# Attention over the memory: the query and output products run by token half, with held weight tiles

## The chip, the cores and the metric

The kernel runs on one core of a Trainium2 chip. The metric is the device time of one execution in microseconds (us), from runs of the whole program; a separate profiled execution gives the trace that is read below. The engines named are PE (TensorE's products; PEld is its loading of the stationary operand), DVE (VectorE), ACT (ScalarE), POOL (GpSimd) and SP (SyncE, which here only issues transfers).

## The reference, cut to what matters

The program is a stack of two models over 256 tokens of width 1024. The first has two layers, and each of them ends its mixer with an attention over a memory of 256 rows, followed by a feed-forward block:

```python
def memory_cross_attention(h, m, w_q, w_kv, q_norm, k_norm, w_o):
    q = rms_norm(to_heads(h @ w_q, XM_HEADS), q_norm)      # h is 256x1024, w_q 1024x512
    k, v = jnp.split(m @ w_kv, 2, axis=-1)
    k = rms_norm(to_heads(k, XM_HEADS), k_norm)
    v = to_heads(v, XM_HEADS)
    sc = jnp.einsum('bhqd,bhkd->bhqk', q, k).astype(jnp.float32) * (XM_HEAD_DIM ** -0.5)
    p = jax.nn.softmax(sc, axis=-1)
    o = jnp.einsum('bhqk,bhkd->bhqd', p.astype(v.dtype), v)
    return from_heads(o) @ w_o                              # w_o is 512x1024
```

There are 4 heads of width 128. `h` is the normed residual stream, and the result is added to the stream `x`. Everything else of the program (two mixers, four feed-forward blocks and the second model) stands before and after it and is not edited.

## The kernel before, in words

**Halves and parts.** The 256 tokens are two halves of 128, h0 and h1 (the loop variable `h` in the code). A matrix product in float32 precision is made from three products of shorter floats: each operand is split into a high and a low part (`xh`, `xl` of the activations, `wh`, `wl` of the weights), and `dense` issues low by high, high by low and high by high for each block of 128 contracted columns. The stationary operand is a 128x128 block of activations, the moving one 512 weight columns.

**Weight tiles.** `weights` loads a tile of two blocks (128x1024 floats, 512 KB) into one of 4 buffers `wr` and splits it: ACT copies the high part (L159), DVE subtracts it from the raw tile for the low part (L160). Without a room of its own the pair goes to the pools `wh` (3 buffers) and `wl` (2 buffers), which all products share. A buffer is free for the next tile when the last product that reads it is done.

**Order in `dense`.** It takes one tile after the other, and for each tile does h0, then h1. Both accumulators (the two PSUM banks `d`) stay open to the last tile, then `done(0)` and `done(1)` are called. A list of rooms, `apart`, changes this for the last `len(apart)` tiles: they are all prepared first, and h0 runs through all of them and calls `done(0)`, and only then h1. A room is a pair of pool names, or None for `wh` and `wl`. Two other places of the kernel use this already.

**The stage.** `memory_attention` norms and transposes `x` (`norm_T`: DVE L292, PE L231, ACT L234, DVE L235, in two column halves i=0 and i=1 for each token half), makes the queries with `dense` on `xm_w_q` (8 blocks, 4 tiles, 24 products for each half) and gives each half to `heads_T`: ACT L819 takes the accumulator, ACT L504 squares it, DVE L506, DVE L243 and POOL L244 make the norm, PE L516 transposes the four heads into the one PSUM bank `t`, and `evac` (ACT L120 or DVE L122) takes them out. Then for h0 and h1, and two heads at a time: scores (PE L480 into a bank `pC0` to `pC3`), the maximum (DVE L563, L566), exponentials (ACT L877), weighing (DVE L704), transposes of the probabilities (PE L757) with their evacuation (ACT L120, DVE L124), and the product with V (PE L480 into the one bank `o`, tile `po`). `split` (ACT L699, DVE L700) takes `po` out into `opK` and `olK`. `out_proj` then multiplies by `xm_w_o` (4 blocks, 2 tiles) for the columns n0=0 and again for n0=512; its `done` (DVE L682) adds the result to `x`. The norm of the feed-forward block follows.

**Buffers.** The layers run in the scopes `m0` and `m1`, which hold 4 buffers of 4 KB a partition under the name `lb4`. In `m0` they carry the two tiles of the memory, two query tiles and a key tile of the mixer; in `m1` the memory and the keys of the four head groups. All of those are read for the last time before the mixer's own output product ends. The feed-forward block's scope lays its own pools over the same bytes: the pools of a scope lie one behind the other in the order in which they are listed.

```python
        "ffn": (dict(g4=2, b2=6, b1=6, b05=2, lb1=1, opX=2, olX=2, op=6, ol=6, wh=4, wl=4, s=10, ls=16),
...
        "m0": (dict(g4=2, b2=6, lb4=4, lb2=7, lb8=1, b1=1, b05=1, chains=4, b2C0=3, b2C1=3, olK=2, b2C3=3, b2O=2, opK=2, b2C2=3,
...
                dict(t=1, o=1, d=2, tK="t", pC0=1, pC1=1, pC2=1, pC3=1, aC0="pC0", tC0="pC0", aC1="pC1", tC1="pC1", aC2="pC2",
```

**What sets the order.** The program is traced in source order, and a list scheduler with its own estimate of durations fixes the order of instructions on each engine when the kernel is built: at each step an engine gets the ready instruction that stands first in the source (a `later` block moves this by so many places). On the chip each engine runs its list in that order and waits where an operand is not there.

Of the kernel before, what the change touches and what calls it, by code (L numbers as in the profile page):

```python
# [487 lines left out]
class Mix1(Core):  # L488
# [187 lines left out]
            filler()  # L676
        self.out_proj(get, I["ab_w_out"][0])

    def out_proj(self, get, w):
        for n0 in (0, 512):  # L680
            def done(h, ps, s=slice(n0, n0 + 512)):
                self.nc.vector.tensor_tensor(self.x[h][:, s], ps, self.x[h][:, s], op=OP.add)  # L682
            self.dense(get, w, n0, 512, done)

    def heads_out(self, och, po, pT, V, heads, d, nb):

# [168 lines left out]
    def memory_attention(self, layer, kv, V):  # L855
        nc, I = self.nc, self.I
        gain = self.row_gain(I["xm_norm"][layer], 1024)

        qg = self.gains_T(I["xm_q_norm"][layer], I["xm_k_norm"][layer], 128)
        qr = [self.l(4) for _ in range(2)]  # L860
        xT = self.norm_T(self.x, gain)
        qT = [self.l(512) for _ in range(2)]
        qv = [t.rearrange("p (h t) -> p h t", h=4) for t in qT]
        self.dense(xT, I["xm_w_q"][layer], 0, 512, lambda h, ps: self.heads_T(ps, xT.r[h], qv[h], qr[h], qg))
        put, get = self.operand(4, [("opK", 4)])
        for h in range(2):
            with self.on("O"):
                po = self.p("o")
            pov = po.rearrange("p (b t) -> p b t", b=4)
            och = Chain(self)  # L870
            for g in (0, 2):
                with self.chain():
                    ps, sv, nmax, pr, pv = self.scores([g, g + 1], lambda i: qv[h][:, i], lambda i: kv[:, i], 256,
                                                       qr[h][:, g:g + 2])
                    sums = self.t(2)
                    for i in range(2):
                        nc.scalar.activation(pv[:, i], sv[:, i], AF.Exp, bias=nmax[:, i:i + 1], scale=qr[h][:, g + i:g + i + 1],  # L877
                                             accum_out=sums[:, i:i + 1])
                    nc.vector.reciprocal(sums, sums)
                    self.weigh(pv, sums)  # L880
                    pT = self.probs_T(h, [pv[:, 0], pv[:, 1]], 2)
                    self.heads_out(och, pov, pT, V, (g, g + 1), 128, 2)
            self.split(put, h, 0, pov)
        self.out_proj(get, I["xm_w_o"][layer])


    def mla(self, filler):
# [1009 lines left out]
```

## Time and profile before

| what | us |
|---|---|
| median of 3 runs (lowest, highest) | 1979.38 (1978.55, 1986.77) |
| the profiled execution, its own time | 1978.56 |
| its span from the first to the last instruction | 1976.9 |
| memory attention of layer 0, from the last query product to the first output product | 365.6 to 382.1 |
| the same of layer 1 | 925.4 to 942.0 |

Places in the trace are given in us from the start of the span. An idle time is given at the instruction that ended it, with the instruction that released it behind an arrow. Products overlap in PE, so that the duration of one is longer than the distance to the next.

### The profile page before, as it was taken

How to read it: one execution, taken by the hardware profiler on the slowest of the kernel's cores; microseconds unless marked ns; L12 is line 12 of the kernel's file. 1: busy time of each engine (PE TensorE's matmuls, PEld its weight loads, DVE VectorE, ACT ScalarE, POOL GpSimd, SP SyncE). 2: the span in 40 equal slices, each digit the busy share in tenths (PEclk: the TensorE clock that was granted, in tenths of full speed). 3: DMA queues.
4: the chain of work that ended last, by engine and by line, in shares of the span. 5: the costliest groups of instructions: out<-in, count | busy, mean ns of one | idle time of the engine just before them, and what ended most of it. 6: DMA issues, size and time to landing. Idle time of an engine off the chain costs nothing.

```text
span 1976.9 us, 35277 instructions
## 1 busy us (share of the span) xinstructions
PE 1889.1 (96%) x14108; PEld 1678.2 (85%) x14108; DVE 1251.0 (63%) x1999; ACT 996.7 (50%) x1611; POOL 191.2 (10%) x270
## 2 busy tenths in 40 slices
PE   8999999899999999899999999998999998998998
PEld 7998778799989987677999888777998796778996
DVE  5665865766566657676666567665555777466555
ACT  5554656554445545665554456453554464434542
POOL 0000401000000001320000013210000214110000
PEclk9999999999999999899999999999999999999999
DMA  7666443466556656234566664313666654025664
GB/s 231 194 214 224 141 144 104 129 199 193 193 194 196 194 195 194 86 107 149 159 193 193 214 152 127 111 44 118 197 194 194 172 163 152 13 75 179 194 193 139
DMA packets 158645, 319.17 MB, mean 161 GB/s; under 512 B 28944, under 2 KB 49680, under 8 KB 158480
## 3 DMA queue, kind: packets, MB, share of 16 engines
q1 hardware_dynamic: 157888, 315.79, 51.0%
q8 instruction: 111, 1.82, 0.4%
q0 software_dynamic: 160, 0.52, 0.1%
q10 hardware_dynamic: 432, 0.60, 0.1%
q14 instruction: 54, 0.44, 0.1%
HBM read 315.82 MB, written 1.05 MB: 160 GB/s over the span
## 4 chain that ended last, share of the span: by engine, by line
PE 47%; DVE 5%; issue 4%; DMA 1%; POOL 1%; ACT 1%; SPq 0%; DVEq 0%; POOLq 0%; ACTq 0%
PE pd L480 21%; PE pd L217 5%; PE pd L218 5%; PE pd L219 5%; PE po L480 2%; PE pr L480 1%; PE ppC L480 1%; DVE wl L160 1%; PE pr L1477 1%; PE pq L1477 1%; PE pg L480 1%; PE pn L480 1%; PE pg L1247 0%; PE pt L516 0%; DMA wr<-in_w_out_dram 0%
## 5 line engine op out<-in xcount | busy, mean ns | idle before, releaser
L160 DVE TENSOR_TENSOR wl<-wr,wh 128x1024 fp32r<-128x1024 f32 (+2 forms) x557 | 675.0, 1214 | 398.6 <-PE pd L218 125.4
L159 ACT ACTIVATE wh<-wr 128x1024 fp32r<-128x1024 f32 (+2 forms) x557 | 584.4, 1051 | 551.8 <-PE pd L480 203.9
L480 PE MATMUL pd<-opX,wl 128*128 128x256 f32 x2112 | 585.3, 278 | 2.1 <-DVE s L243 1.0
L480 PE MATMUL pd<-olX,wh 128*128 128x256 f32 x2112 | 585.1, 277 | 0.3 <-DVE olX L235 0.2
L480 PE MATMUL pd<-opX,wh 128*128 128x256 f32 x2112 | 584.4, 277 | 0.0
L480 PEld LDWEIGHTS pd<-opX,wl 128*128 128x128 f32 x2112 | 398.3, 189 | 2.9 <-ACT opX L234 2.2
L480 PEld LDWEIGHTS pd<-olX,wh 128*128 128x128 f32 x2112 | 398.6, 189 | 0.7 <-DVE olX L235 0.7
L480 PEld LDWEIGHTS pd<-opX,wh 128*128 128x128 f32 x2112 | 398.4, 189 | 0.0
L218 PE MATMUL pd<-wl,op 128*128 128x512 f32 (+4 forms) x952 | 366.8, 386 | 4.5 <-DVE wl L160 4.2
L219 PE MATMUL pd<-wh,op 128*128 128x512 f32 (+4 forms) x952 | 363.0, 382 | 0.0
L217 PE MATMUL pd<-wh,ol 128*128 128x512 f32 (+4 forms) x952 | 342.9, 386 | 6.8 <-DVE ol L235 5.7
L217 PEld LDWEIGHTS pd<-wh,ol 128*128 128x128 f32 x952 | 178.6, 189 | 42.1 <-DVE ol L235 6.9
L218 PEld LDWEIGHTS pd<-wl,op 128*128 128x128 f32 x952 | 179.8, 189 | 40.6 <-DVE wl L160 7.7
L219 PEld LDWEIGHTS pd<-wh,op 128*128 128x128 f32 x952 | 179.7, 189 | 32.5
L244 POOL TENSOR_TENSOR ls<-s,cf 128x1 f32<-128x1 f32 (+2 forms) x30 | 26.6, 887 | 720.9 <-DVE s L243 711.0
L357 DVE TENSOR_TENSOR b<-pd,b 128x256 f32<-128x256 f32 x132 | 55.9, 424 | 62.2 <-ACT b L356 44.2
L244 POOL TENSOR_TENSOR s<-s,cf 128x1 f32<-128x1 f32 (+2 forms) x22 | 22.4, 1019 | 434.2 <-DVE s L243 432.9
L356 ACT ACTIVATE b<-b 128x256 f32<-128x256 f32 x88 | 36.8, 418 | 46.6 <-DVE b L355 46.6
L361 DVE TENSOR_TENSOR ol<-b,op 128x512 fp32r<-128x512 f32 x66 | 45.4, 688 | 18.0 <-ACT op L360 18.0
L360 ACT ACTIVATE op<-b 128x512 fp32r<-128x512 f32 x66 | 41.7, 632 | 21.7 <-DVE b L357 21.1
L355 DVE TENSOR_TENSOR b<-pd,lb 128x256 f32<-128x256 f32 x88 | 37.1, 422 | 13.3 <-PE pd L480 13.3
L300 ACT ACTIVATE b<-x 128x512 f32<-128x512 f32 x32 | 20.2, 630 | 37.7 <-DVE x L375 19.5
(551 smaller groups left out, 2340.0 us busy)
## 6 DMA issues: line engine op xcount, KB each, us to landing
wr<-in_ffn_gu_dram SPq DMA_DIRECT2D x264, 512.0 KB, 4.3
wr<-in_ffn_w_down_dram SPq DMA_DIRECT2D x132, 512.0 KB, 4.3
wr<-in_w_in_dram SPq DMA_DIRECT2D x45, 512.0 KB, 4.4
wr<-in_ab_w_in_dram SPq DMA_DIRECT2D x24, 512.0 KB, 4.1
wr<-in_xm_w_kv_dram SPq DMA_DIRECT2D x16, 512.0 KB, 3.6
wr<-in_w_out_dram SPq DMA_DIRECT2D x16, 512.0 KB, 4.4
wr<-in_ab_w_out_dram SPq DMA_DIRECT2D x8, 512.0 KB, 3.5
wr<-in_xm_w_q_dram SPq DMA_DIRECT2D x8, 512.0 KB, 4.0
```

The lines of the kernel that those rows point to most:

```text
L159: nc.scalar.activation(hi, raw, AF.Copy)
L160: nc.vector.tensor_tensor(lo, raw, hi.bitcast(F32), op=OP.subtract)
L217: nc.tensor.matmul(o, xl, wh[:, k], start=first, stop=False)
L218: nc.tensor.matmul(o, xh, wl[:, k], start=False, stop=False)
L219: nc.tensor.matmul(o, xh, wh[:, k], start=False, stop=last)
L244: self.pow = nc.gpsimd.tensor_tensor(r, a, self.mhalf[:, :n], op=OP.pow)
L355: nc.vector.tensor_tensor(s, ps[:, :256], R, op=OP.mult)
L357: nc.vector.tensor_tensor(y[:, b * 256:b * 256 + 256], ps[:, 256:], s, op=OP.mult)
L360: nc.scalar.activation(hi, yv, AF.Copy)
L361: nc.vector.tensor_tensor(lo, yv, hi.bitcast(F32), op=OP.subtract)
L480: i = self.k.nc.tensor.matmul(out, lhsT, rhs, start=start, stop=stop, skip_group_check=skip)
L1477: last = nc.tensor.matmul(out[rows(c), i], lhs[rows(c), i], rhs[rows(c), i], start=True, stop=True)
```

## The change

The query product gets a room for each of its 4 tiles, so that all of them belong to the group that is held: tiles 0 and 2 of the list go to two `lb4` buffers each, tiles 1 and 3 to `wh` and `wl`. The first half of the tokens runs through all 8 blocks, `heads_T` gets it, then the second half follows. The output product of this stage does the same with its 2 tiles for each of n0=0 and n0=512 (one in `lb4`, one in `wh` and `wl`). `out_proj` is called by the two mixers as well, where `apart` stays empty.

```diff
-    def out_proj(self, get, w):
+    def out_proj(self, get, w, apart=False):
         for n0 in (0, 512):
             def done(h, ps, s=slice(n0, n0 + 512)):
                 self.nc.vector.tensor_tensor(self.x[h][:, s], ps, self.x[h][:, s], op=OP.add)
-            self.dense(get, w, n0, 512, done)
+            self.dense(get, w, n0, 512, done, apart=(("lb4", "lb4"), None) if apart else ())
...
-        self.dense(xT, I["xm_w_q"][layer], 0, 512, lambda h, ps: self.heads_T(ps, xT.r[h], qv[h], qr[h], qg))
+
+        self.dense(xT, I["xm_w_q"][layer], 0, 512, lambda h, ps: self.heads_T(ps, xT.r[h], qv[h], qr[h], qg),
+                   apart=(("lb4", "lb4"), None, ("lb4", "lb4"), None))
...
-        self.out_proj(get, I["xm_w_o"][layer])
+        self.out_proj(get, I["xm_w_o"][layer], True)
```

## Rows read from the trace of the kernel before

**Rows 1.** The page, part 1: busy us, share of the span, instructions.
```profile
PE 1889.1 (96%) x14108; PEld 1678.2 (85%) x14108; DVE 1251.0 (63%) x1999; ACT 996.7 (50%) x1611; POOL 191.2 (10%) x270
```

**Rows 2.** Windows: length, busy us of PE, PEld, DVE, ACT, POOL, granted clock, DMA.
```profile
354.00:365.60 11.60, 11.60 (x57) 9.49 (x56) 8.06 (x14) 7.28 (x12) 1.12 (x2) 1.00 0.66 219
365.60:382.10 16.50, 10.74 (x72) 8.96 (x71) 10.98 (x25) 8.90 (x23) 2.03 (x2) 1.00 0.21 66
...
925.40:942.00 16.60, 10.83 (x73) 8.99 (x71) 11.08 (x25) 8.90 (x23) 2.03 (x2) 1.00 0.20 64
```

**Rows 3.** Waits of PE from 360 to 395 us: total, times, longest.
```profile
PE pt L516 <- ACT lb L120: 1.9, 1, 1.9
PE ppC L757 <- DVE sC L879: 1.7, 1, 1.7
PE po L480 <- DVE olK L700: 1.5, 1, 1.5
PE ppC L757 <- DVE b2C L704: 0.7, 2, 0.5
```

**Rows 4.** Timeline of PE, layer 0: start, us, count, idle before.
```profile
359.99 0.48 PE L217 MATMUL pd<-wh,ol 128*128 128x512 f32 x1
...
365.57 0.60 PE L516 MATMUL pt<-cf,b 128*128 128x128 f32 x4
...
368.58 3.62 PE L480 MATMUL ppC<-lb4K,lb 128*128 128x256 f32 x16
...
376.39 2.05 PE L480 MATMUL po<-b2C,lb2K 128*128 128x128 f32 x16
378.28 0.60 PE L757 MATMUL ppC<-cf,b2C 128*128 128x128 f32 x4
380.35 2.02 PE L480 MATMUL po<-b2C,lb2K 128*128 128x128 f32 x16 [1.47 <-DVE olK L700]
382.13 0.48 PE L217 MATMUL pd<-wh,olK 128*128 128x512 f32 x1
```

**Rows 5.** Timeline of ACT, same stage.
```profile
363.10 0.69 ACT L819 ACTIVATE b<-pd,ls 128x512 f32<-128x512 f32 x1 [1.68 <-PE pd L219]
...
366.41 1.05 ACT L159 ACTIVATE wh<-wr 128x1024 fp32r<-128x1024 f32 x1
367.36 0.68 ACT L120 ACTIVATE lb<-pt,ls 128x512 f32<-128x512 f32 x1
...
371.37 0.56 ACT L877 ACTIVATE b2C<-ppC,sC,ls 128x256 f32<-128x256 f32 x1 [2.81 <-PE ppC L480]
```

**Rows 6.** Timeline of DVE, same stage.
```profile
352.73 0.69 DVE L682 TENSOR_TENSOR x<-pd,x 128x512 f32<-128x512 f32 x1 [0.59 <-PE pd L219]
...
356.59 0.68 DVE L235 TENSOR_TENSOR ol<-ppC,op 128x512 fp32r<-128x512 f32 x1
...
368.59 0.69 DVE L506 TENSOR_REDUCE s<-b 128x4 f32<-128x512 f32 x1 [1.38 <-ACT b L504]
...
376.39 0.69 DVE L704 TENSOR_TENSOR b2C<-b2C,sC 128x512 f32<-128x512 f32 x1
...
379.52 0.68 DVE L700 TENSOR_TENSOR olK<-po,opK 128x512 fp32r<-128x512 f32 x1
...
386.50 2.44 DVE L160 TENSOR_TENSOR wl<-wr,wh 128x1024 fp32r<-128x1024 f32 x2
```

**Rows 7.** Timeline of POOL, same stage.
```profile
367.29 1.02 POOL L244 TENSOR_TENSOR ls<-s,cf 128x4 f32<-128x4 f32 x1 [9.12 <-DVE s L243]
```

**Rows 8.** Timeline of SP's transfer issues before the stage.
```profile
342.31 7.29 SPq L134 DMA_DIRECT2D wr<-in_xm_w_q_dram  x4
```

**Rows 9.** The page, part 6: transfers issued by line, KB each, us to landing.
```profile
wr<-in_xm_w_q_dram SPq DMA_DIRECT2D x8, 512.0 KB, 4.0
```

**Rows 10.** Timeline of PE, the first products of the feed-forward block behind it.
```profile
395.46 0.50 PE L480 MATMUL pd<-opX,wl 128*128 128x256 f32 x2 [0.81 <-ACT opX L234]
396.19 0.38 PE L480 MATMUL pd<-olX,wh 128*128 128x256 f32 x1 [0.23 <-DVE olX L235]
```

## The prediction

> **What bounds the kernel now.** I read the page first: PE is busy for 96% of the span, the next engine, DVE, for 63% [rows 1]. So the time is PE's, and an edit that leaves the number of products alone can only give back time in which PE stands still. The second view was the windows of the two stages that are edited. In the query product PE has no gap (11.60 of 11.60 us), but between it and the output product it works for 10.74 of 16.50 us: 5.76 us of idle time in layer 0, and 16.60 - 10.83 = 5.77 us in layer 1 [rows 2]. The two layers show the same pattern, so I work out layer 0 and double it. The third view, PE's waits, says for what it stands still there: 1.9 us for the evacuation of the transposed queries, 1.7 and 0.7 us for weighed probabilities, 1.5 us for the split of `po` [rows 3]; no output product (L217 to L219) is among these waits, so PE is full there too. Last, the timelines of PE, ACT, DVE, POOL and SP give the chain in its order [rows 4 to 8]. The reader is to see there that both halves of the tokens come out of the query product together (ACT takes h0 at 363.10 us, and the transposes of h0 begin only at 365.57, behind the last product of h1), so that the whole softmax chain runs with no product left to cover it.
>
> **What the change takes away and adds.** Nothing is added to PE, ACT, POOL or the transfers: the same tiles, splits and products, in another order and other buffers. Each part of the order is costed below.
>
> *The pace of products.* 24 products begin between 359.99 and 365.57 us [rows 4]: 5.58 us, or 0.23 us each. A half of the query product is 24 products. It starts at about 354.0: the window of 11.60 us from there holds 57 instructions, the 48 products and two groups of four transposes [rows 2].
>
> *h0 out of the query product earlier.* h0 now ends after 24 products and its own group of transposes (0.60 us, the length of the group at 365.57): 354.0 + 5.6 + 0.6 = 360.2, against 363.10 [rows 4, 5]. That is 2.9 us earlier. Behind it come L819 (0.69), L504 (about as long), the transposes 0.60, an evacuation 0.68, L506 0.69 and POOL's power 1.02 [rows 4 to 7]: 4.4 us even if they all ran one behind the other, under the 5.6 us of h1's products. While POOL has the power, nothing else is queued on POOL in this stage.
>
> *Is h0's operand ready?* Blocks 4 to 7 of h0 need the second column half of `x`, whose operand is complete at 356.59 + 0.68 = 357.27 [rows 6]. Before, 24 products stood ahead of them (h0 and h1 of blocks 0 to 3), now 12: they are due at 354.0 + 12 x 0.23 + 0.6 = 357.4. So it fits with 0.1 us to spare. If it is late by the planner's estimate, products of h1 go ahead, 0 to 12 of them, and h0 ends 0 to 2.8 us later. I take 0, as the measured times fit; the other end is a rival.
>
> *Are the held tiles ready?* SP issues the four query tiles from 342.31 within 7.29 us [rows 8], and they land 4.0 us later [rows 9], so the last by about 354. Two splits no longer wait for `wh` and `wl`, since the `lb4` buffers were read for the last time before the mixer's output product. h0 needs the fourth tile after 18 products, at 358.2 or later. Cost 0; without that cover it would be one split, 1.22 us (two take 2.44) [rows 6].
>
> *The chain behind the query product.* The last query product ends later by h0's four transposes, which now stand among the products: 365.57 + 0.6 = 366.2. The scores of h0 can start there, against 368.58 [rows 4]: 2.4 us earlier. Before, they stood behind the transposes of h1, and these waited for the bank `t`, because ACT did a weight split (366.41) ahead of the evacuation (367.36) [rows 5]. What is late next is DVE. It runs almost without a gap from 368.59 to 376.39 + 0.69 = 377.08, 8.5 us, over the maxima, the norm of h1 and the four weighings [rows 6]; the same instructions stay. They can start when the first two heads' scores are there, a quarter of 3.62 us after 366.2 [rows 4], at 367.1 instead of 368.59, and end at 375.6. So the 2.4 us shrink to 1.5 here.
>
> *From the last weighing to the first output product.* Before, this took from 377.08 to 382.13, 5.05 us [rows 4, 6], because h0's product with V (2.05 us from 376.39) stood on PE ahead of the last transposes (378.28), and h1's product with V waited until DVE had taken h0 out of the single bank `o` (379.52 + 0.68 = 380.20). With h0's half of the chain ahead, both are over by then, and what is left is transposes 0.60, one evacuation 0.68 (priced as the copy out of `po`) and h1's product with V 2.02 [rows 4 to 6]: 3.3 us, and 0.1 us for each of three hand-overs, an estimate from the 0.15 us between 380.20 and 380.35: 3.6 us. The first output product comes at 375.6 + 3.6 = 379.2, against 382.13: 2.9 us earlier. I take these 2.9 us a layer. The lowest value is 0; the highest is all of PE's idle time, 5.76 us.
>
> *The output product.* The 12 products of h0 for n0=0 come first, 2.8 us, which covers h1's split (about 1.3 us: ACT and DVE, 0.7 each). PE is full there as before [rows 3]. The gain is only at its end: h0 is finished 12 products before the end, not 6. Moreover the two late splits, 2.44 us of DVE at 386.50, which stood ahead of the addition for h1 [rows 6], can be done earlier, as two of the four tiles no longer wait for `wl`. The next block's first products now wait 0.81 + 0.23 = 1.04 us for the normed operand [rows 10]; I take 0.5 of it, and 0 to 1.04 as bounds. Against it stands that `opX`, the operand of that block, lies over `lb4` buffers (by the order of the pools, 28 KB into a scope against 20 to 36 KB), so that it may be written only when the output product has read its tiles, 6 products or 1.4 us before the end. In layer 1 it is `olX`. That is still early enough for the first product, so it limits this gain and costs nothing more.
>
> **The sum.** 2 x (2.9 + 0.5) = 6.8 us. Against the profiled execution's own 1978.56 (a span of 1976.9 and 1.7 around it) that gives 1971.8. The median of the runs, 1979.38, is 0.8 above that execution, so I forecast 1972.0. The measurement can tell about 0.5%, 9.9 us, from no change, and this gain is below it.
>
> **The rivals.**
>
> *The banks keep their waits.* The wait of 1.9 us for bank `t` and the one of 1.5 us for bank `o` [rows 3] could turn up again at other places, since each keeps its one bank. Only the 1.7 + 0.7 us for weighed probabilities would go: 2 x 2.4 = 4.8 us, 1973.8. For it: both waits are there in either layer. Against it: they come from two halves that arrive together, and now they arrive 5.6 us apart. Chance 0.14. The Trainium skill, Perfetto Trace Analysis, Identifying Performance Opportunities, says that a gap which repeats on the engine that should be full can mean too little SBUF or PSUM for the next tile; by that rule the order of products would give nothing for these two waits. The rows agree in so far as the two waits do stand at single banks.
>
> *h0 does not come out early.* The scheduler's estimate has the operand of blocks 4 to 7 late and puts up to 12 products of h1 ahead; the change then does not do what it says for the queries. What stays is the output product by halves, whose 12 products of h0 can fill the 1.5 us before h1's product with V, and the 0.5 us: 0.5 to 2 us a layer, 1974.6 to 1977.6, say 1976. For it: 0.1 us is a narrow fit. Chance 0.18.
>
> *All idle time goes.* 2 x (5.76 + 1.04) = 13.6 us, 1965.0 at the best; 1965 to 1969 is this case. It needs DVE to be faster through its 8.5 us, by moving the norm of h1 out of them. Chance 0.13.
>
> *Slower: the splits move into the chain.* Before, two of the four output tiles were split beside the output product, where DVE had time (386.50). With rooms for all four they are ready to go while the chain runs, and an engine that is free for a moment takes them: each one put ahead of a maximum or a weighing delays it by up to 1.22 us on DVE, as the split at 366.41 did on ACT by 0.95 [rows 5, 6]. If two more land so and the chain of h0 gains nothing, it is 2 x 2.44 = 4.9 us slower: 1983.5. It decides from about three splits on the path a layer, when 3 x 1.22 = 3.7 us passes the 3.4 us gained. For it: scores and softmax leave DVE no gap. Against it: between 360 and 366 there is room for four splits (4.9 us) under h1's products. Chance 0.09.
>
> **How the numbers follow.** The forecast, 1969 to 1975, has 0.46. The range reaches up over the rivals with small gains to just above no change, 1979.5, and down to 1966.5; beyond lie about 0.1 (most of the slower rival) and 0.05. Faster by over 0.5% (under 1969.5) is the full recovery and a corner of the forecast: 0.17. Slower by over 0.5% (over 1989.3) needs twice what the slower rival costs: 0.04. The rest, 0.79, is within 0.5%.
>
> **What would show it.** In the trace after: ACT's L819 for h0 some 5 us before L819 for h1; the transposes of the queries of h0 among the query products; PE's idle time between query and output product near 3 us instead of 5.8; no wait of PE for the evacuation of queries; the wait for `po` gone or short. The forecast is wrong if L819 for h0 still comes within 3 us of h1's, if splits (L159, L160) stand between the first maximum and the last weighing, or if PE waits inside either product for a weight tile or for `olX`.

## The result and the profile after

The changed kernel is slower: a median of 1998.83 us (5 runs, 1994.88 to 2001.01) against 1985.41 us for the kernel before in the same session (5 runs, 1978.55 to 1989.44). The ratio is 1.0068, 95% interval 1.0048 to 1.0088: 0.7%, clear of the noise. The forecast was 1972.0, with a range to 1979.5. The profiled execution took 2001.01 us, its span is 1999.3 us (1978.56 and 1976.9 before).

The page, part 1, answers [rows 1]:

```profile
PE 1906.1 (95%) x14108; PEld 1691.8 (85%) x14108; DVE 1252.0 (63%) x1999; ACT 995.9 (50%) x1611; POOL 187.7 (9%) x270
```

The same number of instructions, and of the 22.4 us that the span has grown PE is busy for 17.0: time has come not only from stops but from products that run slower. The windows of the query product, of the stretch behind it in layer 0, and of that stretch in layer 1 answer [rows 2]; the clock is the column of 1.00 and 0.90:

```profile
359.40:373.26 13.86, 12.18 (x57) 9.91 (x57) 7.92 (x15) 7.72 (x13) 1.23 (x3) 1.00 0.64 221
373.26:391.14 17.88, 12.46 (x73) 10.20 (x72) 11.75 (x24) 8.89 (x23) 1.91 (x2) 0.90 0.18 60
...
939.35:955.90 16.55, 10.79 (x73) 9.01 (x72) 11.70 (x24) 8.89 (x23) 1.91 (x2) 1.00 0.18 65
```

The query product, which had no gap before, now takes 13.86 us with 1.68 of idle time. The stretch behind it, up to the first output product at 391.14, still holds 17.88 - 12.46 = 5.42 us of idle time (5.76 before), but its clock is 0.90, and so it is 1.4 us longer than before. In layer 1 it is what it was: 16.55 - 10.79 = 5.76 us of idle time (5.77 before), clock 1.00. PE's longest waits from 340 to 406 us answer [rows 3]:

```profile
PE pt L516 <- ACT lb L120: 1.9, 1, 1.9
PE ppC L757 <- DVE sC L881: 1.8, 2, 1.7
PE pd L217 <- DVE ol L235: 1.7, 1, 1.7
PE po L480 <- DVE olK L700: 1.5, 1, 1.5
PE pd L480 <- ACT opX L234: 0.8, 1, 0.8
PE pd L218 <- DVE wl L160: 0.7, 1, 0.7
...
```

The waits for evacuation, weighed probabilities and `po` are all still there, and two are new: one for the query operand (L235) and one for a low weight tile (L160). PE's timeline, next to [rows 4], shows where:

```profile
353.93 0.50 PE L218 MATMUL pd<-wl,op 128*128 128x512 f32 x1 [0.73 <-DVE wl L160]
...
359.39 0.50 PE L217 MATMUL pd<-lb,ol 128*128 128x512 f32 x1 [0.17 <-DVE x L682]
...
364.96 1.03 PE L231 MATMUL ppC<-cf,b 128*128 128x128 f32 x8
367.68 0.50 PE L217 MATMUL pd<-lb,ol 128*128 128x512 f32 x1 [1.68 <-DVE ol L235]
...
373.26 0.60 PE L516 MATMUL pt<-cf,b 128*128 128x128 f32 x4
375.78 0.66 PE L516 MATMUL pt<-cf,b 128*128 128x128 f32 x4 [1.92 <-ACT lb L120]
376.27 5.30 PE L480 MATMUL ppC<-lb4K,lb 128*128 128x256 f32 x16
```

From 359.39 to 364.96 stand 24 products, 12 of each half over blocks 0 to 3; then all eight transposes of the operand's second column half, a stop, and 24 more. The transposes of the queries begin behind the last product, as before. The 16 scores take 5.30 us, where they took 3.62 [rows 4]. ACT, next to [rows 5]:

```profile
365.25 1.06 ACT L159 ACTIVATE wh<-wr 128x1024 fp32r<-128x1024 f32 x1 [0.61 <-DMA wr<-in_xm_w_o_dram]
366.21 1.06 ACT L234 ACTIVATE op<-ppC 128x512 fp32r<-128x512 f32 x2
370.79 0.69 ACT L819 ACTIVATE b<-pd,ls 128x512 f32<-128x512 f32 x1 [3.52 <-PE pd L219]
...
373.52 0.69 ACT L819 ACTIVATE b<-pd,ls 128x512 f32<-128x512 f32 x1 [0.42 <-PE pd L219]
374.10 1.05 ACT L159 ACTIVATE wh<-wr 128x1024 fp32r<-128x1024 f32 x1
375.05 0.68 ACT L120 ACTIVATE lb<-pt,ls 128x512 f32<-128x512 f32 x1
```

The two halves leave the query product 373.52 - 370.79 = 2.73 us apart, 12 products, not 5 us. They did so before too; this is the line of before that stood behind the first of [rows 5]:

```profile
365.83 0.69 ACT L819 ACTIVATE b<-pd,ls 128x512 f32<-128x512 f32 x1 [0.36 <-PE pd L219]
```

365.83 - 363.10 = 2.73. DVE, next to [rows 6]:

```profile
357.51 1.23 DVE L160 TENSOR_TENSOR lb<-wr,lb 128x1024 fp32r<-128x1024 f32 x1
358.65 0.68 DVE L682 TENSOR_TENSOR x<-pd,x 128x512 f32<-128x512 f32 x1
359.51 1.23 DVE L160 TENSOR_TENSOR wl<-wr,wh 128x1024 fp32r<-128x1024 f32 x1 [0.18 <-ACT wh L159]
360.65 0.68 DVE L682 TENSOR_TENSOR x<-pd,x 128x512 f32<-128x512 f32 x1
361.26 0.68 DVE L292 TENSOR_TENSOR b<-x,g 128x512 f32<-128x512 f32 x1
...
366.94 1.28 DVE L235 TENSOR_TENSOR ol<-ppC,op 128x512 fp32r<-128x512 f32 x2
```

Splits of query tiles now stand in DVE's list ahead of the mixer's last additions to `x` (L682), so that `x`, its norm and the operand come later. In ACT's list splits of both products' tiles stand ahead of L234 and L120, and some of them wait for their transfer (0.61 us at 365.25).

For all that follows the trace of each kernel is cut at the same PE records, counted from the start (2000, 2400, 5000, 5800, 6200, 8000, 9600, 11400, 12850 of 14,108). Each entry is the length of the piece, PE's idle time in it, and the time at half clock (1.2 instead of 2.4 GHz), in us; a piece holds a little more than its stage. "Mixer" is the first model's second mixer, which stands between the two memory stages; 2a and 2b are the two mixers of the second model.

```
                 memory L0        mixer            memory L1      2a               2b
before           77.9  7.5  0     154.4 10.5 10.2  68.8  6.8 0    162.5 15.2 13.7  149.4 19.4 13.7
after            82.4  9.7  3.4   156.4 11.4 10.2  71.7  9.2 0    171.5 18.5 27.3  144.2 15.7 17.1
```

Of the 22.4 us between the two spans these pieces hold 13.2: 7.4 in the memory stages, 2.0 in the mixer, 3.8 in the second model. Most of the rest lies in two feed-forward blocks that ran at another pace (last section). The mixers aren't edited, but the scheduler plans all that comes behind the edit anew: their instructions stand in another order on PE, DVE, ACT and SP, and in the second model on POOL too.

### The profile page after: what moved, and what is told of

It is laid out like the page before. It is cut to its first block, busy times and chain, and to the rows that moved or that the text cites. A ratio compares the mean times of both kernels' runs of the same rounds, so it can differ in the third digit from the quotient of the medians.

```text
span 1999.3 us, 35270 instructions
## 1 busy us (share of the span) xinstructions
PE 1906.1 (95%) x14108; PEld 1691.8 (85%) x14108; DVE 1252.0 (63%) x1999; ACT 995.9 (50%) x1611; POOL 187.7 (9%) x270
## 4 chain that ended last, share of the span: by engine, by line
PE 47%; DVE 5%; issue 4%; DMA 1%; ACT 1%; POOL 1%; SPq 0%; DVEq 0%; POOLq 0%; ACTq 0%
PE pd L480 21%; PE pd L217 5%; PE pd L218 5%; PE pd L219 4%; PE po L480 2%; PE pr L480 1%; PE ppC L480 1%; PE pr L1479 1%; DVE wl L160 1%; PE pq L1479 1%; PE pg L480 1%; PE pg L1249 1%; PE pn L480 1%; PE pt L516 0%; DMA wr<-in_ffn_w_down_dram 0%
## 5 line engine op out<-in xcount | busy, mean ns | idle before, releaser
L160 DVE TENSOR_TENSOR wl<-wr,wh 128x1024 fp32r<-128x1024 f32 (+2 forms) x549 | 665.8, 1215 | 402.0 <-PE pd L480 127.3
L159 ACT ACTIVATE wh<-wr 128x1024 fp32r<-128x1024 f32 (+2 forms) x549 | 575.8, 1050 | 563.3 <-PE pd L480 227.4
L218 PE MATMUL pd<-wl,op 128*128 128x512 f32 (+4 forms) x936 | 360.0, 385 | 6.5 <-DVE wl L160 5.8
L219 PE MATMUL pd<-wh,op 128*128 128x512 f32 (+4 forms) x936 | 356.7, 382 | 0.0
L217 PE MATMUL pd<-wh,ol 128*128 128x512 f32 (+4 forms) x936 | 336.2, 385 | 5.3 <-DVE ol L235 4.3
L218 PEld LDWEIGHTS pd<-wl,op 128*128 128x128 f32 x936 | 176.7, 189 | 43.0 <-DVE wl L160 10.2
L244 POOL TENSOR_TENSOR s<-s,cf 128x1 f32<-128x1 f32 (+2 forms) x22 | 22.4, 1017 | 443.0 <-DVE s L243 441.7
```

Source lines behind the costliest of these rows:

```text
L159: nc.scalar.activation(hi, raw, AF.Copy)
L160: nc.vector.tensor_tensor(lo, raw, hi.bitcast(F32), op=OP.subtract)
L217: nc.tensor.matmul(o, xl, wh[:, k], start=first, stop=False)
L218: nc.tensor.matmul(o, xh, wl[:, k], start=False, stop=False)
L219: nc.tensor.matmul(o, xh, wh[:, k], start=False, stop=last)
L244: self.pow = nc.gpsimd.tensor_tensor(r, a, self.mhalf[:, :n], op=OP.pow)
```

## The experiments

Four theories. A: the held tiles' splits, which stand ahead of the operand and wait for transfers, cost the time, and the query product is the part at fault. B: the output product is. C: the cost lies far away, in the second model's new order. D: it lies in the mixer's new order.

**One part alone, one layer alone.** The list of rooms is left off one of the two products, or given in one layer only (the first shown):

```diff
-        self.out_proj(get, I["xm_w_o"][layer], True)
+        self.out_proj(get, I["xm_w_o"][layer])
```

> The query product is held as in the change, the output product is as before. Theory A (splits in the queues): the cost sits in front of and inside the query product, because the splits of the held tiles stand in ACT's and DVE's order ahead of the mixer's last splits and wait there for their transfers; both layers then show the same shape as the changed kernel (PE waiting 0.7 us for a split and 1.7 us for the normed operand in layer 0), 4 to 5 us a layer, and the time is 8 to 15 us above the kernel before. Theory B (the output product): its held tiles are the cost; then this run is within 3 us of before. Theory C (far away): the stage costs little, and the time is made in the second model, whose instructions are planned in another order; then the stages here are within 2 us of before and the total can lie anywhere between -5 and +10 us.

> The output product is held as in the change, the query product is as before. Theory A: the stages of both layers stay within 1 us of before, and what is left of the difference in total comes from the second model's new order alone. Theory B: 8 to 13 us above before, 4 to 6 a layer. Theory C: stages as before, total between -5 and +10 us.

> Both parts of the change, in layer 0 alone. Theory A: layer 0 loses about 4.5 us as in the changed kernel, the mixer of layer 1 about 1.5 us through its new order, the memory attention of layer 1 nothing; 5 to 8 us in all before the second model. Theory B: about 4.5 us in layer 0, but behind the query product. Theory C: layer 0 within 2 us of before.

> Both products hold their tiles in layer 1 alone; layer 0's memory attention is as in the kernel before. Theory A: layer 0 and the mixer behind it as before (idle 7.5 us), layer 1's memory stage as in after (idle 9.2 us, 2.9 us longer): ratio to before 1.001 to 1.002. Theory C: the mixers of the second model are planned in another order and hold more stops and more time at the lower clock than before (13.7 us in each layer): ratio 1.003 to 1.006, with layer 0's stages unchanged.

Measured: query product alone 1.008 (1.0053 to 1.0107), output product alone 1.0039 (1.0017 to 1.0061), layer 0 alone 1.0069 (1.0043 to 1.0096), layer 1 alone 1.0025 (1.001 to 1.0039). So neither part is free, and B is not the whole. With the output product alone PE waits in a place of its own:

```profile
372.64 0.66 PE L516 MATMUL pt<-cf,b 128*128 128x128 f32 x4 [3.93 <-ACT lb L120]
```

The wait for the evacuation of the queries is 2.0 us longer than before (1.92), because ACT's list has a split for the feed-forward block ahead of it that waits for its transfer:

```profile
370.95 1.06 ACT L159 ACTIVATE wh<-wr 128x1024 fp32r<-128x1024 f32 x1 [1.39 <-DMA wr<-in_ffn_gu_dram]
371.91 0.67 ACT L120 ACTIVATE lb<-pt,ls 128x512 f32<-128x512 f32 x1
```

That is the forecast's slower rival, on ACT instead of DVE. The layers are unequal (0.7% and 0.25%), though the idle time added to their memory stages is much the same, 3.1 and 2.6 us in the two traces. What differs is that only layer 0 has the mixer behind it; that this is the reason is a guess here, theory D below.

**The order in the query product.** `e5_h0_first` puts the first of h1's products behind h0's last (an edge for the order alone, as all edges here); `e4_late_splits` puts the query tiles' splits behind the mixer's last split; `e9_order_back` goes on from it and puts the last two query tiles' splits behind the operand of h0, the output tiles' behind that of h1; `e10_order_h0` adds h0 first to that.

```diff
# h0 first, in dense
-                        nc.tensor.matmul(o, xl, wh[:, k], start=first, stop=False)
+                        m = nc.tensor.matmul(o, xl, wh[:, k], start=first, stop=False)
+                        if before is not None and h and len(apart) == 4 and nw == 512 and apart[0][0] == "lb4":
+                            self.tc.add_manual_dep(m.ins, before.ins.name, mybir.DependencyInfo(mybir.DependencyClass.NoSync, mybir.DependencyReason.DATA), reason="h0 first")
# late splits, in parted
+        for i, j in zip(pair, self.behind or ()):
+            self.tc.add_manual_dep(i.ins, j.ins.name, mybir.DependencyInfo(mybir.DependencyClass.NoSync, mybir.DependencyReason.DATA),
+                                   reason="behind the mixer's last split")
```

> The changed kernel with one more edge: the first product of h1 in the query product stands behind the last product of h0, so that h0 really runs through all 8 blocks first. If an early h0 is worth what was forecast, PE's idle time between the query and the output product falls from 5.8 to about 3 us in either layer, L819 for h0 comes 5 us or more before L819 for h1, and the run is 4 to 7 us faster than the changed kernel. If the operand of blocks 4 to 7 is late instead, PE waits inside the query product for it (2 to 3 us a layer), and the run is within 2 us of the changed kernel.

> After, with one thing more: the splits of the query product's held tiles stand, on ScalarE and on VectorE, behind the mixer's last split (an order on the same engine, no wait). The output product's tiles are split where they were. Theory A (the places of the held tiles' splits in the order cost the time): the waits of TensorE for the mixer's last low tile (0.73 us in layer 0 of after) and for x[h0] (0.17 us) go, and the wait for the second half of the query's operand (1.68 us) stays, since VectorE still makes two splits of the output product's tiles ahead of it. Idle of layer 0's memory stage 9.7 to about 8.9 us; the time 1 to 2 us under after, ratio to before about 1.006. Theory C (the cost lies in the second model, which is planned anew by any edit): no change that can be measured, 1.004 to 1.008. Theory B (the output product is the cost): as after.

> After, with the order of before put back around the norm: the first two tiles of the query product are split behind the mixer's last split, the last two behind the operand's second half of h0, the output product's held tiles behind that of h1, on ScalarE and VectorE. Held tiles and halves stay. Theory A: all extra waits go, the wait for the operand's second half falls from 1.68 to about 0.5 us as before, idle of layer 0's memory stage from 9.7 to 7.5 us and of layer 1's from 9.2 to 7, the clock's fall in the scores of layer 0 (3.4 us at half) goes too, so layer 0's stage takes 78 to 79 us again where after took 82.4: some 7 us under after, ratio to before 1.002 to 1.004 if the second model keeps a cost, 1.000 if it does not. Theory C: the stages of the memory come back, the time does not: 1.005 to 1.008. The products of h0 and h1 still alternate by 12, so none of the 2.9 us of the forecast is to be had.

> The one before, and the query product's first product of h1 held behind the last of h0: the order that the forecast took for granted, with the operand as early as it was before. If the forecast was right but for the order: the idle between query and output product falls from 5.8 to about 3.5 us and the wait for the operand's second half stays near 0.5 us, so each layer's memory stage is 2 us shorter than in the one before, ratio to it 0.998. If the operand is the true limit, because without h1's 12 products in between TensorE reaches blocks 4 to 7 some 2.7 us earlier than before: the wait inside the query product grows to 2 to 3 us, as the 2.38 us in the run with h0 first alone, and the stage is no shorter.

```
                 ratio (interval)           memory L0        mixer            memory L1       2a               2b
e5_h0_first      1.0007 (0.9988 to 1.0027)  82.9  9.8  3.4   150.5 10.7  0    72.5  7.9 3.4   162.6 14.9 13.7  147.4 13.7 23.9
e4_late_splits   1.0078 (1.0058 to 1.0099)  82.1 10.0  3.4   157.4 11.5 13.7  73.2 10.7 0     172.9 19.1 27.3  143.8 13.4 20.5
e9_order_back    1.0020 (1.0000 to 1.0040)  81.9  8.3  6.8   157.1 10.8 13.7  71.1  7.9 3.4   162.3 15.1 17.1  150.7 13.9 27.3
e10_order_h0     1.0059 (1.0039 to 1.0078)  79.9  8.5  0     155.4 11.6  6.8  71.0  8.0 0     172.6 18.6 27.3  142.9 14.7 13.7
```

The last of these is the order that the forecast took for granted, and in it the idle entries between the two products are 0.31, 1.63, 0.44, 0.46 and 0.63, 3.47 us (forecast: near 3). ACT takes h0 at 362.82 and h1 at 368.77, 5.95 us apart (forecast: some 5). But inside the query product PE now waits for the third tile's splits, which had to stand behind the operand:

```profile
358.63 0.50 PE L229 MATMUL pd<-lb,ol 128*128 128x512 f32 x1 [1.20 <-ACT lb L159]
359.89 0.50 PE L232 MATMUL pd<-lb,op 128*128 128x512 f32 x1 [0.76 <-DVE lb L160]
...
372.99 1.99 PE L498 MATMUL ppC<-lb4K,lb 128*128 128x256 f32 x8 [1.63 <-DVE lb L122]
```

1.20 + 0.76 = 1.96 us, most of the 2.29 us gained (5.76 - 3.47). With h0 first alone it is the operand that is late, by 2.38 us:

```profile
361.44 0.54 PE L218 MATMUL pd<-lb,ol 128*128 128x512 f32 x1 [2.38 <-DVE ol L239]
```

The ratios don't follow the memory stages: the kernel with the shortest ones lost 0.59%, the one with h0 first alone nothing. The far pieces differ between these kernels by more than the edit is worth, so the orders had to be held.

**The far orders held.** The order of a stage's instructions on every engine, taken from one built kernel, is given to another as a chain of edges that wait for nothing:

```diff
+                for a, b in zip(order, order[1:]):
+                    self.tc.add_manual_dep(own[b], own[a].name, mybir.DependencyInfo(mybir.DependencyClass.NoSync, mybir.DependencyReason.DATA), reason="order of a plan")
```

> After, unchanged up to the end of the first model; every engine runs the two mixers of the second model in the order that the kernel before has there (issue order alone). So the change's own stages are those of after, and the far ones those of before. Theory A (the cost is in the memory stages, 7.4 us longer in after's profile, and in the mixer between them, 2.0 us longer): the second model comes back to 162.5 and 149.4 us, a loss of 9.0 and a gain of 5.2 us of after goes, and what stays is 9.4 us less what the clock gives by chance: ratio 1.004 to 1.006. Theory C (the far plan is the cost): near 1.000 to 1.002.

> The kernel before, unchanged up to the end of the first model, with the second model's two mixers in the order that after has there: nothing of the change, only its far echo. Theory A: 9.0 us lost in the first of them and 5.2 us won in the second, +3.8 us, ratio 1.001 to 1.003. Theory C: all of the change's loss, 1.005 to 1.008.

> The kernel before with the order of after in the second model's second mixer alone, where three kernels with that order took 142.9 to 144.2 us and before 149.4 us. If that gain belongs to the order: ratio 0.996 to 0.998, faster than both kernels. If it is a chance of the profiled executions: 0.999 to 1.001.

> Held tiles with the order put back and the query product's h0 first (1.0059 in the last call), the second model's first mixer in before's order and its second in after's: the best that was seen of each. By the stages of its profile the kernel it is made from loses 2.0 and 2.2 us in the memory stages and 1.0 us in the mixer between them against before; the first mixer now 10 us shorter than in the kernel it is made from. Ratio 0.999 to 1.001 if the stages add up; 1.003 or more if something else made that kernel slow, as its ratio, above what its stages give, suggests.

```
                       ratio (interval)           memory L0        mixer            memory L1       2a               2b
e11_after_plan_before  1.0058 (1.0037 to 1.0078)  85.4 11.1  6.8   157.0 11.2 13.7  73.4  9.2 3.4   166.7 14.9 23.9  148.9 16.9 20.5
e12_before_plan_after  1.0003 (0.9984 to 1.0021)  78.7  7.0  3.4   150.5 10.8  0    68.9  6.8 0     172.3 19.5 27.3  144.1 14.4 17.1
e13_before_l1_after    0.9943 (0.9919 to 0.9967)  77.9  7.5  0     150.5 10.8  0    68.8  6.8 0     166.0 15.1 20.5  142.3 13.6 17.1
e14_best               1.0002 (0.9978 to 1.0026)  81.6  8.6  3.4   153.5 11.4  3.4  72.6  7.9 3.4   162.7 15.2 13.7  142.5 13.8 17.1
```

C falls as the cause: with the change's whole far echo and nothing of the change (`e12`), the kernel before keeps its time, and with the change and none of its echo in the second model (`e11`) the loss stays, as theory A had it. In `e12` 2a takes 9.8 us more in these pieces, 2b 5.3 us less. The order of 2b alone (`e13`) makes the kernel before 0.57% faster, a median of 1975.81 us against 1985.78. That version beats both kernels, and has nothing of the edit in it. `e12` is `e13` with the order of 2a added and is 0.60% slower: the far echo is small because a gain and a loss of this size cancel. `e14` came to 1.0002, as expected if the stages add up.

**The memory stages alone.** With the mixer and both of the second model's in before's order, a kernel differs from before in the memory stages only. No run held the kernel before to its own order throughout; `g1` below, which holds its second model so and the mixer in after's order, came to 1.0010, so that the holding itself can cost little. `f1` is after, `f2` the run with the order put back, `f5` that with h0 first, `f4` the output product alone.

> After, with the order of before in all three mixers behind layer 0 (the first model's second, and both of the second model): it differs from the kernel before in the two memory stages alone. Theory A (the memory stages cost it): the 1.0058 of the kernel with the second model's order of before stays, 1.004 to 1.006. Theory D (the first model's second mixer, whose order the change moves too, carries it): 1.000 to 1.002.

> The same with the order of before put back around the norm in the memory stages (the splits of the query product's tiles behind the mixer's last split and behind the operand, those of the output product behind the operand). Theory A, with the places of the splits as the mechanism: the waits inside the query product go, the idle time of a stage falls from about 9.5 to 8 us, ratio 1.001 to 1.003. If its 1.0020 of the second call came from the order that it had far away: it stays with the run beside it, 1.004 to 1.006, and the cost of the memory stages is something else that held tiles bring.

> The one before, and h1's products of the query product behind h0's last: the forecast's order. Idle between query and output product 3.5 instead of 5.8 us, but 1.96 us of wait inside the query product for the third tile's splits, as in the trace with h0 first in the second call, where both memory stages took 2.0 and 2.2 us more than before. If that trace tells it all: 1.001 to 1.003. If something follows the stage that its idle time does not show (1.0059 there, and 1.0059 between the two runs of the third call that differ in the memory stages and the mixer between): 1.004 to 1.006.

> Held tiles and halves in the output product alone, with the order of before in the three mixers. By the trace of the same edit without the order of before, the evacuation of the queries waits behind two more splits on ScalarE, 3.9 instead of 1.9 us in each layer: +4 us, ratio 1.002. Theory A sees the query product as the greater cost: 1.002 against 1.005 for both. If the output product carries it alone: 1.004 or more.

Measured: 1.0018 (1.0001 to 1.0035), 1.0027 (1.001 to 1.0044), 1.0016 (0.9994 to 1.0038), 1.0031 (1.0014 to 1.0047). `f1` lies where theory D had it (1.000 to 1.002) and below theory A's 1.004 to 1.006. The four can't be told apart, so A in its narrow form falls: putting the splits back gains nothing that can be measured. The pieces, with those of the two runs of the next paragraph:

```
                       memory L0        mixer            memory L1       2a               2b
f1_after_pinned        83.0 10.2  3.4   154.4 10.5 10.2  72.7  8.4 3.4   165.5 15.2 20.5  149.2 18.0 17.1
f2_order_back_pinned   81.5  9.4  3.4   150.5 10.8  0    72.1  8.3 3.4   162.0 15.0 13.7  150.6 18.7 17.1
f5_order_h0_pinned     80.3  8.9  0     150.5 10.8  0    72.5  8.0 3.4   165.3 15.3 20.5  152.6 18.1 23.9
f4_output_pinned       81.3  9.0  3.4   152.1 10.8  3.4  72.7  8.8 3.4   163.6 14.7 17.1  152.2 16.9 27.3
g1_before_mla_after    79.3  7.2  3.4   157.2 11.0 13.7  68.9  6.8 0     164.6 14.8 17.1  151.1 19.8 20.5
g2_after_mla_before    84.6 10.1  6.8   154.4 10.5 10.2  69.8  7.5 0     172.3 17.7 30.7  142.9 13.5 17.1
```

In all four f kernels PE stands still longer in the memory stages than in before (7.5 + 6.8 us): by 4.3, 3.4, 2.6 and 3.5 us together, where the ratios stand for 3.2 to 6.2 us. The waits of PE in layer 0 say what for. In `f1`:

```profile
PE pd L217 <- DVE ol L235: 2.2, 1, 2.2
PE pt L516 <- ACT lb L120: 1.9, 1, 1.9
```

and in `f2`, where the wait for the operand is gone:

```profile
PE pt L530 <- ACT lb L120: 4.0, 1, 4.0
```

The wait for the evacuation has grown by 2.1 us (L530 and L516 are the same line of the code). In ACT's list a split for the feed-forward block stands ahead of it that waits for its transfer, as with the output product alone, and ahead of that one an output tile's split, which waited for its own transfer:

```profile
367.10 1.06 ACT L159 ACTIVATE wh<-wr 128x1024 fp32r<-128x1024 f32 x1 [0.94 <-DMA wr<-in_xm_w_o_dram]
...
369.19 1.06 ACT L159 ACTIVATE wh<-wr 128x1024 fp32r<-128x1024 f32 x1 [0.46 <-DMA wr<-in_ffn_gu_dram]
370.15 0.67 ACT L120 ACTIVATE lb<-pt,ls 128x512 f32<-128x512 f32 x1
```

No run put these splits behind the evacuation, so what held tiles would cost in that order stays open.

**The mixer alone.**

> The kernel before, with the order of after in the first model's second mixer alone (the one that stands between the two memory stages): nothing of the change, and no other stage in another order. Theory D (this mixer's order carries most of the loss): the trace shows a third stop, about 0.7 us before a score product, behind the two that are there anyway, then a stretch of 3 to 10 us at half clock, and the ratio is 1.003 to 1.005. Theory A (the memory stages alone carry it): 0.999 to 1.001, and the run of the fourth call that left this mixer in before's order (1.0018) is a chance.

> After, with the order of before in that mixer alone; memory stages and second model as in after. Theory D: what is left is the memory stages' 0.2% and the second model's 0.0%, ratio 1.001 to 1.003. Theory A: 1.005 to 1.007, as after.

Measured: 1.0010 (0.9993 to 1.0026) and 1.0054 (1.0033 to 1.0076). D falls as the greater part: the first is below its 1.003 to 1.005, the second above its 1.001 to 1.003; both lie where theory A had them. (`g2` does not leave the memory stages wholly as in after: with the mixer held, layer 1's came out with 7.5 us of idle time, 9.2 in after.) The third stop (0.68 us) and 3.4 us of half clock behind it did show in the first, so what theory D looked for is there, but it is worth little (last section).

## Why the prediction was wrong

**The step that failed** is *Is h0's operand ready?*. It read the loop of `dense` as the order of execution ("before, 24 products stood ahead of them, now 12") and took 0 late products out of a bound of 0 to 12. On the chip the scheduler's order counts, and it ran 12 products of h0, 12 of h1, 12 and 12 in either kernel: L819 came 2.73 us apart before and after. That is within 3 us, the first of the prediction's own signs of being wrong. [Rows 5] were printed for 363.10 but not for the line of h1 at 365.83, which would have shown it. *H0 out of the query product earlier*, *the chain* and *from the last weighing to the first output product* rest on it, and with it the 2.9 us a layer. It was the rival "h0 does not come out early", at 0.18, but with the wrong price: no gain came from the output product by halves, whose first 12 products of h0 already ran ahead of h1's (in before the addition for h0, L682, starts at 385.16, 12 products behind 382.13).

**What showed the mechanism right:** with h0 first by force, the idle time between the products fell from 5.76 to 3.47 us (forecast: near 3). Most of that gain was paid inside the query product. The 0.1 us to spare did not exist, however. Counted back from 359.63, the query product of before begins at 353.67, not 354.0, and the 13th product from there, where h0's second half would stand, at 356.89, ahead of the operand at 357.27:

```profile
353.67 0.39 PE L217 MATMUL pd<-wh,ol 128*128 128x512 f32 x1
...
356.89 0.39 PE L217 MATMUL pd<-wh,ol 128*128 128x512 f32 x1
```

Forced, the operand came 2.38 us late, and, with the splits out of its way, the third tile's splits 1.96 us late.

**Are the held tiles ready? Cost 0** was wrong as well. The step looked at when tiles are ready for PE, not at what stands behind their splits. Without the wait for `wh` and `wl`, the scheduler puts splits ahead of the last additions to `x`, and a split that waits for its transfer holds all that is behind it: 0.73 + 0.17 + 1.68 us of PE in layer 0. The slower rival (0.09) had this on DVE behind the query product, at 1983.5; the runs showed it on ACT there (a wait of 1.92 us grew to 3.93) or ahead of the operand. In the sum itself there is a slip as well: 1979.38 - 6.8 is 1972.6, not 1972.0.

**What no step had:** an edit moves the order of stages that it doesn't touch, and part of the loss goes with the clock. Six kernels hold the memory stages, the mixer and the second model in all the needed combinations: after 6.8, `f1` 1.8, `e11` 5.8, `g1` 1.0, `e12` 0.3 and `g2` 5.4 thousandths above before. If the three parts add, their least squares are 3.2 for the memory stages, 1.8 for the mixer and 1.3 for the second model, each with an error of 0.7, or 6.4, 3.6 and 2.6 us (the last two are more than `g1` and `e12` show by themselves, 1.0 and 0.3). `f1` lies 1.4 below that sum, so a part may also depend on the others; how the loss is shared stays open to that extent. That the memory stages carry a loss, and that the output product's tiles alone suffice for it (`f4`), is measured.

Part of it goes with the clock. Its mean was 0.9832 in the five runs of after and 0.9868 in 134 runs of before, and from run to run of one kernel 0.001 of clock goes with 1.3 us (a line through all kernels' runs with a level for each): 0.0036 stands for 4.7 us of the 13.4, an estimate. The loss of `f1` is not of this kind: its mean clock is that of before in the same session, 0.9865. In the trace of after it shows in layer 0: PE stood still for 1.68 and 1.92 us, and the stretch behind was at 0.75, with 3.4 us at half clock:

```profile
373.00:376.40 3.40, 1.48 (x11) 1.12 (x10) 2.55 (x4) 2.82 (x5) 1.01 (x1) 1.00 0.25 49
376.40:383.20 6.80, 5.18 (x17) 3.91 (x15) 5.10 (x14) 2.82 (x11) 1.01 (x1) 0.75 0.34 131
```

In layer 1 the same two stops, 1.68 and 1.92 us, as far apart, were followed by no fall (clock 1.00 from 939.35 on), and `e12` and `g1`, whose layer 0 stands in before's order, have 3.4 us at half clock there. So the stops alone do not decide it, and what does is open.

The start of the next block in layer 0 waited 0.76 + 0.22 us where 0.81 + 0.23 stood before [rows 10], and in layer 1 for 0.76 + 0.34 us, where 0.96 stood: the 0.5 us a layer forecast there did not come.

## What to carry to other kernels

Read the order of execution from the trace or the built program before pricing a change of loops: where a scheduler orders the instructions, two source orders can give the same one. A buffer that is waited for also keeps its producer out of the way; take the wait away and ask what the freed instruction will now stand in front of, on each engine. Hold the order of the untouched stages when a change is to be judged by less than a per cent, and look at that order as a thing to tune: here one mixer's order was worth 0.57%, more than the 0.34% (6.8 us) that the edit was forecast to bring.

## What the runs showed of the hardware

**Two paces at full clock.** PE's windows in the first and the last feed-forward block, in before and then in after, show the same products, no idle time and clock 1.00:

```profile
40.00:90.00 50.00, 50.00 (x444) 50.00 (x443) 31.71 (x41) 25.51 (x32) 0.00 (x0) 1.00 0.62 192
1850.00:1890.00 40.00, 40.00 (x356) 40.00 (x355) 22.94 (x28) 20.41 (x27) 0.00 (x0) 1.00 0.63 194
```

```profile
40.00:90.00 50.00, 50.00 (x427) 50.00 (x426) 31.16 (x41) 25.13 (x32) 0.00 (x0) 1.00 0.59 186
1870.00:1910.00 40.00, 40.00 (x342) 40.00 (x341) 21.99 (x25) 19.57 (x27) 0.00 (x0) 1.00 0.61 185
```

444 against 427 products in 50 us, 4% apart, 0.113 and 0.117 us each, constant through the block. It changes from block to block and execution to execution: the fastest kernel of this study has 427 in the first window and the quick pace in the last block. One such block is worth 4 to 5 us; two of them are 9 of the 22.4 us between the two profiled spans, and no part of the change. The Trainium skill, TensorE: Matmul & The Clock Gate, section "Wait — 56ns, not 53.3ns?", gives a product at full clock its columns at 2.4 GHz and about 2.5 ns more. That is 0.109 us for 256 columns, an estimate from that page; both paces measured here are above it, and the measurement decides. Why there are two is open.

**A short third stop and the clock.** In the mixer PE stops twice in either order, for 2.1 and 0.6 to 0.8 us. In the order of after a third stop of 0.68 us follows. The run with after's mixer alone (`g1`), its stops, and the windows behind the third one:

```profile
844.75 0.61 PE L516 MATMUL pt<-cf,b 128*96 128x128 f32 x4 [2.08 <-DVE b L539]
847.20 0.64 PE L516 MATMUL pt<-cf,b 128*96 128x128 f32 x4 [0.81 <-DVE s L966]
848.52 0.49 PE L480 MATMUL ppC<-lb,b 96*128 96x128 f32 x2 [0.68 <-ACT lb L120]
```

```profile
848.50:850.10 1.60, 1.58 (x9) 1.14 (x9) 0.94 (x3) 0.96 (x2) 1.20 (x3) 1.00 0.00 0
850.10:853.50 3.40, 3.40 (x13) 2.74 (x13) 2.09 (x7) 1.34 (x7) 1.03 (x1) 0.50 0.00 0
```

and the same place in the fastest kernel, in before's order:

```profile
844.69 0.61 PE L516 MATMUL pt<-cf,b 128*96 128x128 f32 x4 [2.10 <-DVE b L539]
847.14 0.64 PE L516 MATMUL pt<-cf,b 128*96 128x128 f32 x4 [0.82 <-DVE s L243]
```

```profile
848.20:854.20 6.00, 6.00 (x32) 4.21 (x30) 4.48 (x10) 3.33 (x12) 2.24 (x4) 1.00 0.00 0
```

All nine traces with the third stop have 3.4 to 10.2 us at half clock at this place, and none of the eleven without it has any. In seven of the nine the clock fell 1.1 to 1.9 us after the third stop had ended, as here. In the other two (`e11` and `e3_layer0_only`, with 10.2 us each) it fell 1.3 and 1.5 us after the first stop had ended, ahead of the second and the third, so there the third stop did not bring it. The two go together; that the third stop is the cause is not shown. Half of such a time is lost where PE has work throughout: in the seven 1.7 to 3.4 us, an estimate from 3.4 to 6.8 us at half clock, beside the 1.8 thousandths (3.6 us) of the sum above. Elsewhere in the mixer the clock falls or not from one execution to the next of the same order: stretches of 3.4 and 6.8 us in before, none in `e12` and `e13`, and the piece took 154.4 or 150.5 us.
